# First two modulation vectors of a decoder block by quarters: sums moved from VectorE to TensorE, first norm on two engines, three projections begun quarter by quarter

## The chip, the core and the metric

One core of a Trainium2 chip runs the whole program. The metric is device time in microseconds (us) of one execution; less is better.

## The reference, cut to what matters

The program is one decoder block over 512 tokens of width 1024: adaLN modulation, two token mixers, an expert mixer and norms. The change touches only its beginning:

```python
mod = silu(c) @ w_ada + b_ada                      # c (1024), w_ada (1024, 6*1024)
shift1, scale1, gate1, shift2, scale2, gate2 = split(mod, 6)
h = rms_norm(x, norm1_w) * (1.0 + scale1) + shift1 # x (512, 1024)
proj = h @ w_in                                    # w_in (1024, 2320)
aq, ak, av, gq, gk, gv, gg, glr = split(proj)      # 512,128,128,256,256,512,512,16
log_a = log_sigmoid(glr @ gla_gate_up + gla_gate_bias) / 16
# then sliding-window attention, gated linear attention, w_out, residual,
# second norm, expert retrieval, residual, final norm
```

`h` needs all of `x` and, for each block of 128 of its 1024 columns, the same 128 columns of `scale1` and `shift1`. Everything after it is a product with `h`.

## The kernel before

All tensors have 128 partitions; a 1024-wide vector is 8 blocks (`KD`), numbered k = 0 to 7. Work is emitted in program order and a scheduler then fixes one order for each engine's queue; each queue runs strictly in that order.

The front of the program is this. SyncE (SP) issues the loads: `x` in eight pieces of 256 KB, then the columns of `w_ada` for vectors 1 (`scale1`) and 0 (`shift1`) in halves of 512 columns, 2 MB a half, and between them 1 MB groups of `w_in` (`wi3`, `wi4`, ...; group 3 is `gq`, group 4 `gk`, 0 to 2 the attention's q, k, v). The tiles of the ring `raw` (three of 1 MB) and tiles that are free so early (`qT`, `mixA`) take them.

ScalarE (ACT) squares and scales `x` (lines 233 and 237), and TensorE (PE) transposes it (`xt`, line 246; "x_transposes"). `mod_half(v, half)` makes a half of a modulation vector: VectorE (DVE) sums the 8 blocks of rows, each times `silu(c)` (`scs`), into `macc`, by one instruction of 128x512 for each block (lines 267, 269); PE then sums `macc` over the partitions by four products with a column of ones (`mt`, line 273); DVE adds the bias (`modT`, line 275) and makes `aT`, the scale of the norm (line 278).

With `aT` and `modT`, ACT turns each transposed block into `h` (line 298) and rounds it to `hTh`; DVE subtracts for the rest, `hTl` (line 302). The weights are split in the same way, `wi_0h`, `wi_1h` on ACT (line 59) and `wi_0l`, `wi_1l` on DVE (line 60), `_0` for k = 0 to 3 and `_1` for k = 4 to 7, in rings of three. A product in full precision is then three matmuls for each k (`mm3`, lines 64 to 66).

The projections are emitted in the order: the decay's gate (`decays`, accumulator `pglr`), groups 3, 4, 0, 1, 2 (`proj_T`, accumulators `pj`, two for each group: `pj30` is group 3's first). That is eleven accumulators of 8 x 3 = 24 matmuls of 512 columns, 264 in all, before the first matmul of the linear attention (`pa`, lines 474 to 493). From 340 us on, the expert mixer fills the rest of the span.

Of the kernel before, what the change touches and what calls it, by code (L numbers as in the profile page):

```python
# [17 lines left out]
P = 128  # L18
D = 1024
# [22 lines left out]
def peer_block_kernel(ctx: ExitStack, tc: tile.TileContext, a: dict, out: bass.AP):  # L42
# [9 lines left out]
    def raw(shape, name):  # L52
        return st.tile(shape, F32, tag="raw", bufs=3, name=name)
# [63 lines left out]
    def bank(name, tag="m"):  # L117
        return banks["pool"].tile([P, 512], F32, tag=tag, bufs=BUFS[tag], name=name)

    def bank2(name):  # L120
        return psf.tile([P, 2, 512], F32, tag="sc2", bufs=1, name=name)

    def pbank(name):
        return ps.tile([P, 512], F32, tag="ph", name=name)
# [104 lines left out]
    for n in range(NT):  # L229
        sq = frA.tile([P, D], F32, tag="m4", bufs=2, name=f"sqa{n}")  # L230
        ss = frA.tile([P, 2], F32, tag="ss", bufs=2, name=f"ssa{n}")
        for q in range(2):
            nc.scalar.activation(sq[:, q * 512:(q + 1) * 512], xn[n][q], AF.Square, accum_out=ss[:, q:q + 1])
        nc.vector.tensor_tensor(ss[:, 0:1], ss[:, 0:1], ss[:, 1:2], OP.add)
        r = rstd_of(frA, ss[:, 0:1], float(D), 1, f"ra{n}")
        for q in range(2):
            nc.scalar.activation(xn[n][q], xn[n][q], AF.Copy, scale=r)
    xts = []

    def x_transposes(ks):  # L240
        for k in ks:
            if k % 4 == 0:
                x_transposes.two = bank2(f"xt{k}")
            pt = x_transposes.two[:, k % 4] if k % 4 < 2 else bank(f"xt{k}", ("pt", "po")[k % 2])
            for n in range(NT):
                nc.tensor.transpose(pt[:, n * P:(n + 1) * P], xn[n][k // 4][:, k % 4 * P:(k % 4 + 1) * P], ident)
            xts.append(pt)

    x_transposes(range(4))
    hTh = frA.tile([P, KD, T], FR, name="hTh")  # L250
    hTl = frA.tile([P, KD, T], FR, name="hTl")

    mtb = bank("mt")

    def mod_half(v, half):
        acc = frA.tile([P, D], F32, tag="m4", bufs=2, name=f"macc{v}{half}")[:, :512]
        c0 = v * D + half * 512
        if v == 1:
            parts = [(raw([P, 4, 512], f"wa{half}{i}"), 4) for i in range(2)]
        else:  # L260
            parts = [(qT, 4)] + [(t.rearrange("p a b -> p (a b)")[:, None, :], 1) for t in mixA]
        k = 0
        for w, nk in parts:
            nc.sync.dma_start(w, a["w_ada"][k * P:(k + nk) * P, c0:c0 + 512].rearrange("(k p) d -> p k d", p=P))
            for i in range(nk):
                if k == 0:
                    nc.vector.tensor_scalar(acc, w[:, i, :], scs[:, 0:1], None, op0=OP.mult)
                else:
                    nc.vector.scalar_tensor_tensor(acc, w[:, i, :], scs[:, k:k + 1], acc, op0=OP.mult, op1=OP.add)
                k += 1  # L270
        pb = mtb[:, 16 * v + 4 * half:16 * v + 4 * half + 4]
        for i in range(4):
            nc.tensor.matmul(pb[:, i:i + 1], acc[:, i * P:(i + 1) * P], ones[:, 0:1], start=True, stop=True)
        cs = slice(v * 8 + 4 * half, v * 8 + 4 * half + 4)
        nc.vector.tensor_tensor(modT[:, cs], pb[:, 0:4], badaT[:, cs], OP.add)
        if v == 1:
            hs = slice(4 * half, 4 * half + 4)
            nc.vector.scalar_tensor_tensor(aT[:, 0, hs], modT[:, cs], 1.0, n1T[:, hs], op0=OP.add, op1=OP.mult)

# [6 lines left out]
    for half in range(2):  # L286
        mod_half(1, half)
        if half == 1:
            fetch(a["w_in"][4], 4, 256, "wi")
        mod_half(0, half)  # L290
        if half == 0:
            fetch(a["w_in"][3], 3, 256, "wi")
        else:
            x_transposes(range(4, KD))
        for k in range(4 * half, 4 * half + 4):
            h32 = frA.tile([P, T], F32, tag="h32", bufs=4, name=f"h32_{k}")
            if k < KD - 1:
                nc.scalar.activation(h32, xts[k], AF.Identity, bias=modT[:, k:k + 1], scale=aT[:, 0, k:k + 1])
            else:
                nc.vector.tensor_scalar(h32, xts[k], aT[:, 0, k:k + 1], modT[:, k:k + 1], op0=OP.mult, op1=OP.add)  # L300
            nc.scalar.activation(hTh[:, k, :], h32, AF.Copy)
            nc.vector.tensor_tensor(hTl[:, k, :], h32, hTh[:, k, :], OP.subtract)
    wg = frA.tile([P, KD, 16], F32, name="wg")
    nc.sync.dma_start(wg, a["w_glr"])
# [46 lines left out]
    def decays():  # L351

        pg = pbank("pglr")
        for k in range(KD):
            mm3(pg[:16, :], wgh[:, k, :], wgl[:, k, :], hTh[:, k, :], hTl[:, k, :], k == 0, k == KD - 1)
        nc.scalar.activation(glrT, pg[:16, :], AF.Copy)
        for j in range(2):
            pz = bank(f"pz{j}", ("pt", "po")[j])
# [208 lines left out]
    proj_T(4, [[t[:, :, j, :] for t in gk] for j in range(2)], bank)  # L567
# [523 lines left out]
def layouts(inp):  # L1091
# [6 lines left out]
    o["w_ada"] = c(g["w_ada"][0])  # L1098
    o["b_ada"] = c(g["b_ada"])
# [48 lines left out]
```

## Time and profile before

| what | value |
|---|---|
| median of 3 runs | 1557.18 us (1555.11 to 1562.12) |
| the profiled execution | 1555.13 us, of which its span 1553.4 us |
| TensorE busy | 1493.2 us (96%) |
| VectorE busy | 1251.8 us (81%) |
| ScalarE busy | 688.8 us (44%) |
| DMA | 409.67 MB, mean 264 GB/s |

Times inside the program are counted from the start of the span. A busy PE in these rows is not a PE at its best: matmuls overlap, so the distance between the starts of two matmuls is what one costs, and the length printed for one is longer. "idle before" stands behind a row with what ended the wait.

### The profile page before, as it was taken

The numbers are of one execution on the slowest core, as the hardware profiler recorded it, in microseconds if no ns is written. First come the engines' busy times: TensorE is split into PE (matmuls) and PEld (weight loads), VectorE is DVE, ScalarE is ACT, GpSimd is POOL, SyncE is SP. The second block draws the span as 40 slices with busy tenths as digits, with TensorE's granted clock in tenths as the row PEclk, the third lists the DMA queues.
The fourth block names the chain that finished last, engine by engine and source line by source line (L and its number), as shares of the span: only waits on it lengthen the run. The fifth ranks groups of instructions, "written<-read, shape, count | busy, mean of one in ns | idle before, by whom it ended". The sixth has DMA issues, their size and how long they took to land.

```text
span 1553.4 us, 24408 instructions
## 1 busy us (share of the span) xinstructions
PE 1493.2 (96%) x9379; PEld 1328.2 (86%) x9379; DVE 1251.8 (81%) x2476; ACT 688.8 (44%) x1078; POOL 412.9 (27%) x327
## 2 busy tenths in 40 slices
PE   4999989899999999999999999999999999999996
PEld 3787878888998999999888888888888888888885
DVE  7578668589989898995678778878888878887997
ACT  5545576433445666564333333333333333333343
POOL 1000000144500000003243334433434434434550
PEclk9999999999999999999999999999999999999998
DMA  9253444262346677679998999888998989898893
GB/s 349 89 204 131 171 142 173 108 239 92 127 155 188 198 239 235 201 239 388 380 348 317 339 348 346 322 340 333 364 330 329 338 340 354 326 340 334 292 331 129
DMA packets 154932, 409.67 MB, mean 264 GB/s; under 512 B 10288, under 2 KB 77120, under 8 KB 142400
## 3 DMA queue, kind: packets, MB, share of 16 engines
q1 hardware_dynamic: 108736, 261.30, 47.2%
q0 software_dynamic: 36864, 134.23, 23.0%
q10 hardware_dynamic: 9216, 12.59, 2.2%
q8 instruction: 73, 1.20, 0.3%
q14 instruction: 43, 0.35, 0.1%
HBM read 366.14 MB, written 41.94 MB: 263 GB/s over the span
## 4 chain that ended last, share of the span: by engine, by line
PE 63%; DVE 3%; DMA 2%; ACT 1%; issue 1%; DVEq 0%; ACTq 0%; SPq 0%
PE acc L65 11%; PE acc L64 11%; PE acc L66 11%; PE ph L66 8%; PE ph L64 8%; PE ph L65 8%; PE pg L874 4%; DMA Gd<-gs 1%; DMA gr<-Gd 1%; DVE o L867 1%; ACT gs L876 0%; DVE o L862 0%; DVE oh L819 0%; DVE oh L822 0%; DVE oh L817 0%
## 5 line engine op out<-in xcount | busy, mean ns | idle before, releaser
L887 POOL DMA_INDIRECT gu<-in_u_dram,ix_u x128 | 170.2, 1329 | 531.5 <-PE pg L874 273.5
L897 POOL DMA_INDIRECT gv<-in_vP_dram,ix_v x128 | 171.0, 1336 | 214.9 <-DVE gu L889 183.1
L902 DVE SCALAR_TENSOR_TENSOR gacc<-gv,hg,gacc 128x1024 f32<-128x1024 f32 x127 | 162.7, 1281 | 3.3 <-DMA gv<-in_vP_dram,ix_v 3.1
L889 DVE SCALAR_TENSOR_TENSOR gu<-gu,h2n 128x1024 f32<-128x1024 f32 x128 | 156.0, 1219 | 5.9 <-DMA gu<-in_u_dram,ix_u 5.9
L1028 ACT ACTIVATE Ah<-ge 128x384 fp32r<-128x384 f32 x64 | 33.6, 525 | 155.1 <-PE acc L65 155.1
L1028 ACT ACTIVATE Ah<-gel 128x384 fp32r<-128x384 f32 x64 | 33.6, 525 | 154.4 <-PE acc L65 154.4
L876 ACT ACTIVATE gs<-pg 128x512 f32<-128x512 f32 x96 | 94.3, 1108 | 9.8 <-PE pg L874 9.8
L867 DVE TENSOR_TENSOR o<-o,gp 128x1024 bf16<-128x1024 bf16 x144 | 91.0, 687 | 4.3
L874 PE MATMUL pg<-o,o 128*128 128x128 bf16 x1152 | 79.3, 223 | 5.3 <-DVE o L867 5.3
L874 PEld LDWEIGHTS <-o 128*128 128x128 bf16 x1152 | 69.7, 99 | 14.4 <-issue 8.5
L953 POOL IOTA iot<- 128x256 bf16 x1 | 1.5, 1541 | 282.8 <-DVE h2Tl L675 282.8
L1029 DVE TENSOR_TENSOR Al<-gel,Ah 128x384 fp32r<-128x384 f32 x64 | 35.6, 556 | 45.2 <-ACT Ah L1028 45.2
L699 ACT ACTIVATE ge<-ph 128x384 f32<-128x384 f32 x128 | 60.8, 475 | 23.8 <-PE ph L66 23.7
L862 DVE TENSOR_TENSOR o<-iot,t 128x2048 bf16<-128x2048 bf16 x48 | 58.5, 1218 | 4.9 <-ACT t L842 4.9
L1029 DVE TENSOR_TENSOR Al<-ge,Ah 128x384 fp32r<-128x384 f32 x64 | 35.5, 555 | 19.2 <-ACT Ah L1028 18.1
L1024 DVE TENSOR_TENSOR ge<-ge,gr 128x384 f32<-128x384 f32 x64 | 35.4, 553 | 10.9 <-ACT ge L699 10.9
L212 DVE SCALAR_TENSOR_TENSOR macc<-wa,scs,macc 128x1024 f32<-128x1024 f32 x28 | 39.0, 1392 | 4.9 <-DMA wa<-in_w_ada_dram 4.7
L1024 DVE TENSOR_TENSOR gel<-gel,gr 128x384 f32<-128x384 f32 x64 | 32.8, 553 | 0.0
L65 PE MATMUL pq<-h2Tl,wq_0h 128*128 128x512 f32 (+1 forms) x80 | 27.9, 349 | 1.2 <-DVE h2Tl L675 1.2
L64 PE MATMUL pq<-h2Th,wq_0h 128*128 128x512 f32 (+1 forms) x80 | 28.0, 352 | 1.0 <-ACT qha L751 1.0
L65 PE MATMUL pq<-h2Tl,wq_1h 128*128 128x512 f32 (+1 forms) x80 | 28.2, 353 | 0.0
L66 PE MATMUL pq<-h2Th,wq_1l 128*128 128x512 f32 (+1 forms) x80 | 28.2, 352 | 0.0
(2599 smaller groups left out, 5077.1 us busy)
## 6 DMA issues: line engine op xcount, KB each, us to landing
u<-in_uT_dram SPq DMA_DIRECT2D x64, 1024.0 KB
v<-in_vP_dram SPq DMA_DIRECT2D x64, 1024.0 KB
Gd<-gs SPq DMA_DIRECT2D x24, 1024.0 KB
gr<-Gd SPq DMA_DIRECT2D x16, 1536.0 KB
wa<-in_w_ada_dram SPq DMA_DIRECT2D x20, 1024.0 KB
gsp<-ge ACTq DMA_DIRECT2D x64, 192.0 KB
gel<-gsp SPq DMA_DIRECT2D x32, 384.0 KB
wi<-in_w_in_dram SPq DMA_DIRECT2D x9, 1024.0 KB
```

Of the source, the lines that this page charges most:

```text
L64: nc.tensor.matmul(acc, lh, rh, start=start, stop=False)
L65: nc.tensor.matmul(acc, lh, rl, start=False, stop=False)
L66: nc.tensor.matmul(acc, ll, rh, start=False, stop=stop)
L867: nc.vector.tensor_tensor(o2[:, :, m], o12[:, :, 1], gp3[:, g0:g0 + H, m, None].to_broadcast([P, H, P, 2]), OP.mult)
L874: nc.tensor.matmul(pt[:, i, :], o12[:, g, 0, :, r], o2[:, g, m, :, r], start=(m == 0), stop=(m == 2))
L876: nc.scalar.activation(gs[:, :, t0 + 4 * f:t0 + 4 * f + 4].rearrange("p b a -> p a b"), pt, AF.Copy)
L887: nc.gpsimd.indirect_dma_start(out=ur, out_offset=None, in_=a["u"], in_offset=bass.IndirectOffsetOnAxis(ap=ix_u[:, s:s + 1], axis=0))
L889: nc.vector.scalar_tensor_tensor(ur, ur, 1.0, h2n, op0=OP.mult, op1=OP.mult, accum_out=hid[:, s:s + 1])
L897: nc.gpsimd.indirect_dma_start(out=vr, out_offset=None, in_=a["vP"], in_offset=bass.IndirectOffsetOnAxis(ap=ix_v[:, s:s + 1], axis=0))
L902: nc.vector.scalar_tensor_tensor(gacc, vr, hg[:, s:s + 1], gacc, op0=OP.mult, op1=OP.add)
L1024: nc.vector.tensor_tensor(ge, ge, v_part.g[:, :, c % CG, :], OP.mult)
L1029: nc.vector.tensor_tensor(Al, gef, Ah, OP.subtract)
```

## The change

The columns of vectors 0 and 1 are laid out anew in memory, in quarters of 256 columns, so that a quarter is 1 MB with 8 KB in a row for each partition (`w_ada01`). Each vector is made by quarters (`mod_quarter`). A quarter q gives the two blocks k = 2q and 2q+1. For vector 0 and for the first quarter of vector 1, PE multiplies the raw weights with `scs`: 16 products of a 128x128 piece with one column, and DVE only adds the bias. For the other three quarters of vector 1, DVE sums as before, with 256 columns instead of 512, and PE does two products with ones. Of the first norm, DVE takes the second square and the first scaling. Transposes come by quarters in one pair of banks (`bank2`). The accumulators of the gate and of `proj_T(4)` change banks, so that the gate, `pj30`, `pj31`, `pj40` and `pj41` can all be open while the quarters arrive.

```diff
+    def mod_quarter(v, q, on_vector):
+        w = quarter.pop((v, q))
+        pb = mtb[:, 8 * v + 2 * q:8 * v + 2 * q + 2]
+        if on_vector:
+            acc = frA.tile([P, D], F32, tag="m4", bufs=2, name=f"macc{v}{q}")[:, :256]
+            nc.vector.tensor_scalar(acc, w[0], scs[:, 0:1], None, op0=OP.mult)
+            for k in range(1, KD):
+                nc.vector.scalar_tensor_tensor(acc, w[k], scs[:, k:k + 1], acc, op0=OP.mult, op1=OP.add)
+            for i in range(2):
+                nc.tensor.matmul(pb[:, i:i + 1], acc[:, i * P:(i + 1) * P], ones[:, 0:1], start=True, stop=True)
+        else:
+            for i in range(2):
+                for k in range(KD):
+                    nc.tensor.matmul(pb[:, i:i + 1], w[k][:, i * P:(i + 1) * P], scs[:, k:k + 1], start=(k == 0),
+                                     stop=(k == KD - 1))
...
+    fetch_quarter(1, 0, "A")
+    fetch_quarter(0, 0, "B")
+    fetch(a["w_in"][3], 3, 256, "wi")
+    fetch_quarter(1, 1, "C")
+    fetch_quarter(0, 1, "D")
...
+    fetch(a["w_in"][4], 4, 256, "wi")
+    fetch_quarter(1, 2, None)
...
-        for q in range(2):
-            nc.scalar.activation(sq[:, q * 512:(q + 1) * 512], xn[n][q], AF.Square, accum_out=ss[:, q:q + 1])
+        nc.scalar.activation(sq[:, 0:512], xn[n][0], AF.Square, accum_out=ss[:, 0:1])
+        nc.vector.scalar_tensor_tensor(sq[:, 512:1024], xn[n][1], 1.0, xn[n][1], op0=OP.mult, op1=OP.mult,
+                                       accum_out=ss[:, 1:2])
...
+    for q in range(4):
+        two = bank2(f"xt{q}")
+        for i in range(2):
+            k = 2 * q + i
+            for n in range(NT):
+                nc.tensor.transpose(two[:, i, n * P:(n + 1) * P], xn[n][k // 4][:, k % 4 * P:(k % 4 + 1) * P], ident)
+        mod_quarter(1, q, q > 0)
+        mod_quarter(0, q, False)
+        if q == 0:
+            fetch_quarter(0, 2, "A")
+            fetch_quarter(1, 3, "B")
+        elif q == 1:
+            fetch_quarter(0, 3, "C")
...
-    proj_T(4, [[t[:, :, j, :] for t in gk] for j in range(2)], bank)
+    proj_T(4, [[t[:, :, j, :] for t in gk] for j in range(2)], lambda name: bank(name, ("pt", "po")[int(name[-1])]))
```

What this does to the queues shows at three places. The first is PE's queue of the kernel before, where its matmuls with `h` begin. `xt6` and `xt7` are transposes of k = 6 and 7, `macc11` is the second half of vector 1; a row's numbers behind the names are those of the buffers.

```order
L246 MATMUL xt4_372<-ident_73,Eg_113 128x128 x8
L246 MATMUL xt6_381<-ident_73,Eg_113 128x128 x4
L246 MATMUL xt7_386<-ident_73,Eg_113 128x128 x4
L64 MATMUL pglr_416<-hTh_273,wgh_409 16x512
L64 MATMUL pj30_470<-hTh_273,wi3_0h_462 128x512
L65 MATMUL pglr_416<-hTl_274,wgh_409 16x512
```

All 32 transposes stand ahead of the first matmul with `h`, and of the sums over partitions (`mt`) 8 of 16 products.

The same place of PE's queue in the changed kernel, from the first matmul with `h` on; line 302 is now the transposes, line 265 the products with one column.

```order
L64 MATMUL pglr_485<-hTh_277,wgh_478 16x512
L64 MATMUL pj30_538<-hTh_277,wi3_0h_530 128x512
L64 MATMUL pj31_565<-hTh_277,wi3_0h_530 128x512
L64 MATMUL pj40_600<-hTh_277,wi4_0h_592 128x512
L64 MATMUL pj41_627<-hTh_277,wi4_0h_592 128x512
L302 MATMUL xt1_336<-ident_73,gv0_109 128x128
L302 MATMUL xt1_336<-ident_73,gv1_110 128x128
L302 MATMUL xt1_336<-ident_73,gv2_111 128x128
L302 MATMUL xt1_336<-ident_73,gv3_112 128x128
```

Behind the first five matmuls stand the eight transposes of quarter 1 and then 16 products of its vector 0; the quarters 2 and 3 follow in the same way between matmuls, so that 24 transposes and 48 products now stand behind the first matmul with `h`.

The second is one of these stretches, later in the same queue (`Eg` holds quarter 3 of vector 0).

```order
L64 MATMUL pj31_565<-hTh_277,wi3_1h_534 128x512
L65 MATMUL pj31_565<-hTl_278,wi3_1h_534 128x512
L265 MATMUL mt_276<-scs_86,Eg_113 128x1 x16
L66 MATMUL pj31_565<-hTh_277,wi3_1l_535 128x512
L64 MATMUL pj31_565<-hTh_277,wi3_1h_534 128x512
```

The 16 products stand in the middle of `pj31`, and the next matmul waits until PE has done them.

The third is DVE's queue of the changed kernel ahead of the first `h` (`macc11` and `macc12` are quarters 1 and 2 of vector 1, `wi4_0l` the lower part of `wi4`).

```order
L259 SCALAR_TENSOR_TENSOR macc11_345<-Eg_113,scs_86,macc11_345 128x256 x2
L60 TENSOR_TENSOR wi4_0l_593<-wi4_204,wi4_0h_592 128x1024
L268 TENSOR_TENSOR modT_83<-mt_276,vec_69 128x2
L257 TENSOR_SCALAR macc12_393<-wa12_206,scs_86 128x256
L314 TENSOR_SCALAR h32_1_332<-xt0_279,aT_85,modT_83 128x512
```

The bias of vector 0's first quarter (`modT`), without which there is no `h`, stands behind the split of `wi4`, and so behind that load.

On ACT, the split of `wi0` (its first half, `wi0_0h`), which needs a free place in the ring of three, now stands ahead of `h` of k = 6.

## Rows read from the trace of the kernel before

**Rows 1.** The page's busy time of PE, with its share of the span, and the clock granted to PE in 40 slices of the span.

```profile
PE 1493.2 (96%) x9379; PEld 1328.2 (86%) x9379; DVE 1251.8 (81%) x2476; ACT 688.8 (44%) x1078; POOL 412.9 (27%) x327
PEclk9999999999999999999999999999999999999998
```

**Rows 2.** Busy time by stretch: from:to and length in us, then busy us (and instructions) of PE, PEld (its weight loads), DVE, ACT, POOL, the granted clock, the DMA share and GB/s.

```profile
0.00:33.80 33.80, 11.16 (x49) 9.80 (x49) 24.83 (x80) 19.72 (x45) 4.89 (x21) 1.00 0.94 338
33.80:46.60 12.80, 10.99 (x55) 7.70 (x53) 10.02 (x18) 1.08 (x2) 0.00 (x0) 1.00 0.67 272
46.60:101.80 55.20, 55.20 (x249) 42.55 (x249) 35.34 (x55) 30.77 (x42) 0.00 (x0) 1.00 0.33 112
101.80:340.00 238.20, 225.24 (x2242) 191.82 (x2242) 171.25 (x463) 132.65 (x293) 20.30 (x10) 0.99 0.46 165
340.00:1553.40 1213.40, 1190.59 (x6791) 1076.31 (x6789) 1010.37 (x1863) 504.55 (x698) 387.70 (x297) 0.99 0.79 288
```

**Rows 3.** PE in order of time, from its first matmul with `h` to the first `pa` and one wait later: start, length, engine, line, what is written and read, count, and the idle time before it with what ended it. Between the rows at 65.27 and 70.71 lie 24 matmul starts.

```profile
33.79 0.78 PE L64 MATMUL pglr<-hTh,wgh 128*16 128x512 f32 x1
39.92 0.95 PE L273 MATMUL mt<-ones,macc 128*128 128x1 f32 x8
40.73 0.48 PE L64 MATMUL pj<-hTh,wi_0h 128*128 128x512 f32 x1
43.00 0.50 PE L66 MATMUL pj<-hTh,wi_0l 128*128 128x512 f32 x1 [1.56 <-DVE wi_0l L60]
45.40 0.95 PE L273 MATMUL mt<-ones,macc 128*128 128x1 f32 x8
46.60 0.50 PE L64 MATMUL pj<-hTh,wi_0h 128*128 128x512 f32 x1 [0.26 <-DVE modT L275]
...
60.05 1.98 PE L359 MATMUL pz<-glrT,gup 16*128 16x512 f32 x4
65.27 0.39 PE L66 MATMUL pj<-hTh,wi_1l 128*128 128x512 f32 x1
70.71 0.39 PE L66 MATMUL pj<-hTh,wi_0l 128*128 128x512 f32 x1
101.80 0.32 PE L477 MATMUL pa<-Eg 64*32 64x32 f32 x8
149.63 0.21 PE L493 MATMUL pa<-gq,gk 64*32 64x32 f32 x1 [2.11 <-issue]
```

**Rows 4.** PE in order of time: products with one column and transposes, and the row that follows where the distance is read. One product of 128x128 with one column is two records (16 products of `mt` in lines 273 are 32 records).

```profile
20.80 1.71 PE L273 MATMUL mt<-ones,macc 128*128 128x1 f32 x8
26.21 1.87 PE L273 MATMUL mt<-ones,macc 128*128 128x1 f32 x8 [3.70 <-DVE macc L269]
30.46 3.67 PE L246 MATMUL xt<-ident,Eg 128*128 128x128 f32 x16 [2.39 <-ACT h L298]
105.01 0.60 PE L575 MATMUL pv<-ident,vT 128*128 128x128 f32 x4
105.44 0.27 PE L384 MATMUL sc<-am,identb 128*128 128x256 bf16 x1
156.15 1.84 PE L224 MATMUL mt<-ones,macc 128*128 128x1 f32 x16
157.85 0.38 PE L384 MATMUL sc<-am,identb 128*128 128x512 bf16 x1
```

**Rows 5.** ACT in order of time: the split of `wi3` as it lands, and `h` and `hTh` of the first half.

```profile
25.20 1.06 ACT L59 ACTIVATE wi_0h<-wi 128x1024 fp32r<-128x1024 f32 x1 [5.38 <-DMA wi<-in_w_in_dram]
28.96 2.79 ACT L298 ACTIVATE h<-xt,modT,aT 128x512 f32<-128x512 f32 x4 [1.56 <-DVE modT L275]
31.63 2.19 ACT L301 ACTIVATE hTh<-h 128x512 fp32r<-128x512 f32 x4
```

**Rows 6.** DVE in order of time: three blocks of a half's sum, the lower part of `wi3`, and a bias.

```profile
17.92 2.33 DVE L269 SCALAR_TENSOR_TENSOR macc<-wa,scs,macc 128x512 f32<-128x512 f32 x3
26.29 1.23 DVE L60 TENSOR_TENSOR wi_0l<-wi,wi_0h 128x1024 fp32r<-128x1024 f32 x1
28.77 0.15 DVE L275 TENSOR_TENSOR modT<-mt,vec 128x4 f32<-128x4 f32 x1
```

**Rows 7.** Busy time by stretch, columns as in rows 2, while the first loads run.

```profile
10.00:20.00 10.00, 3.45 (x13) 2.25 (x14) 6.82 (x25) 7.34 (x19) 0.00 (x0) 1.00 1.05 392
20.00:30.00 10.00, 4.38 (x21) 4.20 (x19) 9.65 (x17) 3.24 (x5) 0.00 (x0) 1.00 1.05 389
30.00:40.00 10.00, 9.54 (x42) 7.19 (x42) 9.79 (x16) 4.88 (x8) 0.00 (x0) 1.00 1.04 408
```

**Rows 8.** Busy time by stretch, columns as in rows 2, behind the wait of 2.11 us in rows 3.

```profile
150.00:151.00 1.00, 1.00 (x9) 0.97 (x9) 1.00 (x2) 0.26 (x1) 0.00 (x0) 0.94 0.82 315
151.00:152.00 1.00, 1.00 (x7) 1.00 (x6) 1.00 (x2) 0.34 (x1) 0.00 (x0) 0.50 0.04 12
153.00:154.00 1.00, 1.00 (x6) 1.00 (x6) 1.00 (x4) 0.97 (x5) 0.00 (x0) 0.50 0.65 147
154.00:155.00 1.00, 1.00 (x11) 0.87 (x12) 1.00 (x2) 1.00 (x6) 0.00 (x0) 0.85 1.06 438
```

**Rows 9.** What PE waited for from 101.8 to 340 us, the longest: us in total, times, longest.

```profile
PE pa L493 <- issue: 2.8, 2, 2.1
PE pn L64 <- ACT Eg L348: 1.6, 1, 1.6
```

## What I expected, before the changed kernel was run

> **What bounds the kernel now.** I read the page first: TensorE (PE) is busy 96% of the span [rows 1], so what counts is where PE stands still, or does work that it need not do. The table of stretches says where [rows 2]: PE is busy 11.2 of the first 33.8 us, 11.0 of the next 12.8, all of the 55.2 us from 46.6 to 101.8, 225 of 238 us to 340, and 1191 of 1213 us after that. So PE waits for the rest of the machine only until 46.6 us; from there the front of the program is a PE queue. Anything that puts more work into that queue, or takes some out, moves the end by as much, unless one of the few later waits takes it up.
>
> The timeline of PE over this stretch [rows 3] gives the yardstick. PE starts with `h` at 33.79 and reaches `pa` at 101.80, 68.0 us later. The 264 matmuls of 512 columns in between cost 5.44 us / 24 = 0.2267 us each, 59.85 us together. All else in these 68.0 us is 8.15 us: the two groups of `mt` and their surroundings, the wait of 1.56 for `wi_0l`, the two `pz` (1.98), a slow first microsecond. The old way thus wastes little once it has begun: what there was to win is the 33.8 us before, and some 4 us of waits and sums behind them.
>
> **When PE starts in the changed kernel.** The loads bind until then: 389 to 408 GB/s in every stretch of ten us [rows 7]. Before, `wi3` is the seventh megabyte in line (2 of `x`, 4 of `w_ada`, itself), and ACT starts on it as it lands, at 25.20 [rows 5]. In the new order the seventh megabyte is quarter 1 of vector 0, and `wi4` follows with the small `wg` ahead of it: 1.11 MB more, 2.8 us at 390 GB/s, so 28.0; I take 27.6, since half of the new pieces lie 8 KB in a row and the rate was 408 where more such groups ran. Then come in line, by the queues shown with the change: ACT's split of `wi4` (1.06 long, about 1.0 until the next) [rows 5], DVE's lower part (1.23, about 1.1), the bias (0.15) [rows 6], `h` (2.79/4 = 0.70) and `hTh` (2.19/4 = 0.55) [rows 5], and some 0.3 for four hand-overs. Together 3.8: PE begins with `h` at 31.4, 2.4 us earlier than before. DVE's and ACT's work is hidden behind the loads otherwise: the four squares and scalings that DVE takes over lie before 20 us, and the sums of vector 0 that it loses (two halves of 8 instructions, 0.75 to 0.78 each [rows 6], some 12 us) did not sit ahead of PE after 46.6. Of the waits only 1.56 + 0.26 [rows 3] go with them.
>
> **What PE's queue then holds.** The same 264 matmuls, 59.85. Of the transposes, 24 instead of none. They cost 0.11 each where PE runs at its upper clock ((105.44 - 105.01)/4) and 0.23 where it doesn't (3.67/16) [rows 4]; at the upper level 2.6 us. Then 48 products with one column (three quarters of vector 0, 16 each). The trace has such products: `mt` at 156.15, 8 products in 16 records, is followed 1.70 us later, so 0.2125 each; earlier, at 20.80 and 26.21, 4 took 1.71 and 1.87, so 0.45 [rows 4]. At the upper level the 48 are 10.2 us. Two sums with ones, two products each: 0.85. The two `pz`: 1.9. One new wait: ACT's split of `wi0` needs a place in the ring that PE frees only in the middle of quarter 3, and `h` of k = 6 stands behind it on ACT; by my count PE comes to that `h` some 1.0 us before it is there (0 to 2). Sum beside the 264: 16.55 against 8.15, so 8.4 us more, less the 2.4 of the earlier start: **6.0 us later at `pa`**, with PE at its upper clock throughout. I checked the other side of each step on the way: quarter 3 of vector 1 is the last load; 5.4 MB behind `wi4` at 400 GB/s it lands near 41, and its `h` is wanted by PE some 20 us later (31.4 and the two thirds of 27.2 + 16.6 that stand ahead of it), so no load is late for PE any more. That is the point of the change, and it is paid with PE time.
>
> **The clock.** [...] The granted column reads 1.00 before 34 us, but the transposes at 30.46 and the products at 20.80 cost twice what the same forms cost at 105 and 156 [rows 4], so this is the lower level. Later the column shows one fall: after a standstill of 2.11 us [rows 3] it reads 0.50 at 151 to 154 and is back in the slice after [rows 8]: some 3.4 us at half pace, 1.7 us lost. In the changed kernel PE does only products and eight transposes, with gaps between loads, until 31.4, so I expect it to start low: five matmuls at 0.43 and eight transposes at 0.23 instead of 0.2267 and 0.11 are 2.0 us more. Whether a stretch of 16 products keeps PE up, no row shows: the longest in the trace is the 1.70 us at 156, with no fall. Bounds for each of the three stretches: nothing, or 16 x (0.45 - 0.2125) = 3.8 in it and 1.7 behind it. That gives 0 to 2.0 + 3 x 5.5 = 18.5 us in all. I take 5.0: the slow start, and one stretch of the three, for a stretch of 3.4 us with hardly a column streaming is nearer to the standstill than to the matmuls around it, yet lies between full work.
>
> **Sum.** 6.0 + 5.0 = 11.0 us later at `pa`. From 101.8 to 340 us PE stands 13 us, and nearly all of these waits are for results that PE's own queue feeds (the longest that are not are 1.6 us for ACT and the 2.8 of "issue" [rows 9]); I let none of it absorb the delay, 4 at most. The profiled execution of 1555.13 (span 1553.4) becomes 1566.1; it lies 2 below the median 1557.18, which becomes **1568**. This measurement can tell about 0.5%, 7.8 us, from no change.
>
> **Rivals.**
> A, the forecast: PE's queue grows, 1562 to 1575, **0.5**.
>
> B, the clock falls in every stretch. Then up to 6.0 + 18.5 = 24.5 us, 1575 to 1582. For it: the fall after 2.11 us of standstill [rows 8]. Against it: no fall after 1.70 us of products. **0.15**. [...]
>
> C, no change: the delay is taken up after `pa`. DVE has 12 us less to do early, the scheduler's order between 100 and 230 us differs in many places, and waits there could shrink. At +4 or less the result is 1555 to 1562, **0.2**. Against it: nothing before 340 us but PE is near its limit (DVE 171 of 238 us, ACT 133 [rows 2]).
>
> D, faster: the products cost PE nothing, because their weight loads slip behind the 512-column matmuls around them (PEld is busy only 42.6 of 55.2 us there [rows 2]). The sum beside the 264 falls to some 3.8 with transposes free too: 31.4 + 63.6 = 95.0, 6.8 us earlier than before, 1550; with waits after `pa` shrinking too, 1544. It decides at the price of a product: below 4.2/48 = 0.088 us the change wins, above it loses. The row says 0.2125, inside dense work [rows 4]. [...] **0.15**, which also holds what I don't see in the new order.
>
> **Numbers.** 1568 is A. A's own range is 1562 to 1575; the range 1553 to 1580 takes in C, most of B and the upper half of A's absorption, and leaves out D and the ends. Faster by over 0.5% (below 1549): part of D, 0.12. Slower by over 0.5% (above 1565): B and most of A, 0.6. Within 0.5%: 0.28.
>
> **What would show it.** In the profile after: PE's first matmul with `h` between 30 and 33; the three groups of 32 records of one-column products at 3.4 us each or up to 7; hardly any wait of PE from there to `pa`; `pa` at 107 to 115. `pa` before 101.8 refutes the sum. With `pa` at 108 or later and an end that is not later, C holds. I am wrong if the products are cheaper than 0.1 us, if PE starts with `h` before 28, or if PE waits for loads in the middle.

## The result, and the profile after

The changed kernel takes 1576.49 us (median of 5 runs, 1575.72 to 1576.91) against 1557.18 before: ratio 1.0119, 95% interval 1.0103 to 1.0135, so slower by 19.3 us. The profiled execution took 1576.91, its span is 1575.1; before it was 1553.4, so the two traces differ by 21.7. Of e6, one of the kernels further down, two executions took 3810 and 8377 us; they are left out of its median and ratio.

The page of after, PE's busy time and granted clock, answers to [rows 1]: PE is busy 27 us more, a point more of a longer span, and the clock's second slice is now an 8.

```profile
PE 1520.2 (97%) x9519; PEld 1353.0 (86%) x9519; DVE 1250.2 (79%) x2489; ACT 678.9 (43%) x1060; POOL 408.3 (26%) x327
PEclk9899999999999999999999999999999999999999
```

The stretches of after, columns as in [rows 2], cut at PE's first matmul with `h`, at the first `pa` (right behind the last `pj`), and at the first `ph`. That is an early matmul of the expert mixer: its work on PE begins with `pq`, some 24 us ahead of `ph`, and so well before the 340 us named at the head of this document. Under them the last two stretches of before, cut at the same places (the first of its stretches, 33.79 to 101.80, can be read from [rows 3]).

```profile
31.67:117.09 85.42, 85.42 (x397) 68.50 (x397) 44.86 (x84) 33.74 (x45) 0.00 (x0) 0.92 0.31 113
117.09:317.70 200.61, 185.89 (x1998) 154.26 (x1998) 139.49 (x310) 112.00 (x266) 1.87 (x2) 0.97 0.43 149
317.70:1575.10 1257.40, 1231.74 (x7052) 1114.02 (x7050) 1045.10 (x2019) 520.12 (x722) 401.80 (x304) 0.99 0.79 286
```

```profile
101.80:295.90 194.10, 181.14 (x1983) 151.69 (x1983) 136.60 (x307) 116.65 (x269) 1.87 (x2) 0.98 0.43 152
295.90:1553.40 1257.50, 1234.69 (x7052) 1116.44 (x7050) 1045.01 (x2019) 520.55 (x722) 406.13 (x304) 0.99 0.79 286
```

So there are two losses and no third. In the **front**, PE starts 2.1 us earlier, needs 85.4 instead of 68.0 us for the eleven accumulators, and is done 15.3 later. In the **middle**, up to the first `ph`, another 6.5 are lost (200.6 against 194.1), 1.8 of them with PE standing (14.72 against 12.96) and 4.8 with PE busy longer over nearly the same matmuls (1998 and 1983 records). Behind `ph` nothing moves (1257.4 and 1257.5).

PE of after in order of time, answering to [rows 3]: the products of the first quarter of vector 0, ahead of `h`; the start; the three stretches of products with the row that follows each; and the first `pa` behind the last `pj`. The last row is DVE's: the bias of that first quarter.

```profile
22.96 6.98 PE L265 MATMUL mt<-scs,mixA 128*128 128x1 f32 x32 [0.73 <-DVE modT L268]
...
31.67 0.61 PE L64 MATMUL pglr<-hTh,wgh 128*16 128x512 f32 x1 [0.46 <-ACT hTh L317]
32.07 1.91 PE L64 MATMUL pj<-hTh,wi_0h 128*128 128x512 f32 x4
33.78 1.91 PE L302 MATMUL xt<-ident,gv 128*128 128x128 f32 x8
35.48 1.39 PE L265 MATMUL mt<-scs,wakl 128*128 128x1 f32 x8
...
39.41 0.39 PE L65 MATMUL pglr<-hTl,wgh 128*16 128x512 f32 x1
...
50.00 3.65 PE L265 MATMUL mt<-scs,qT 128*128 128x1 f32 x32
53.51 0.77 PE L66 MATMUL pj<-hTh,wi_0l 128*128 128x512 f32 x1
...
64.27 4.23 PE L265 MATMUL mt<-scs,Eg 128*128 128x1 f32 x32
68.36 0.77 PE L66 MATMUL pj<-hTh,wi_1l 128*128 128x512 f32 x1
...
117.09 0.45 PE L489 MATMUL pa<-Eg 64*64 64x64 f32 x8
...
29.98 0.16 DVE L268 TENSOR_TENSOR modT<-mt,vec 128x2 f32<-128x2 f32 x1 [0.42 <-PE mt L265]
```

The three stretches take 3.93, 3.51 and 4.09 us, 11.53 together. Around the first and the third, by stretch, columns as in [rows 2]; PE is busy all the time.

```profile
38.00:39.00 1.00, 1.00 (x11) 1.00 (x11) 0.00 (x0) 0.00 (x0) 0.00 (x0) 1.00 1.09 414
40.00:43.00 3.00, 3.00 (x9) 1.95 (x8) 2.35 (x6) 1.89 (x3) 0.00 (x0) 0.50 0.36 147
43.00:44.00 1.00, 1.00 (x6) 0.82 (x5) 0.96 (x3) 0.00 (x0) 0.00 (x0) 0.89 0.00 0
66.00:67.00 1.00, 1.00 (x11) 1.00 (x11) 0.00 (x0) 0.00 (x0) 0.00 (x0) 1.00 0.00 0
70.00:73.00 3.00, 3.00 (x8) 2.32 (x8) 1.64 (x3) 0.80 (x2) 0.00 (x0) 0.50 0.00 0
74.00:75.00 1.00, 1.00 (x6) 0.73 (x5) 0.66 (x1) 0.00 (x0) 0.00 (x0) 1.00 0.00 0
```

The granted clock (the last column but two) reads 1.00 within the products and drops to 0.50 around their end: the matmuls of 512 columns behind them then stand 0.43 apart instead of 0.2267, and pay for it. [Rows 8] showed such a fall behind a standstill of 2.11 us; here there is no standstill at all. The front adds up: 59.85 for the 264 matmuls, 11.53 for the products, 3.32 for 24 transposes (1.70 + 0.79 + 0.83), 0.72 for two sums, 2.10 for two `pz`, 0.98 for the first five matmuls (2.11 us, 0.42 apart instead of 0.2267); that is 78.50 of 85.42. The remaining 6.9 are the falls; the clock column gives the same, (1 - 0.92) x 85.42 = 6.8. (It reads 1.00 in the slow start, so it holds the falls alone.)

In the middle, the longest wait of after is new: `gb`, the sum of the third modulation vector, waits 4.3 us for ACT's copy `gv` ([rows 9] have none such). PE, then ACT in order of time, then two stretches.

```profile
150.82 2.08 PE L219 MATMUL gb<-macc,ones 128*128 128x512 f32 x2 [4.27 <-ACT gv L362]
...
146.90 3.60 ACT L461 ACTIVATE Eg<-Eg 128x4096 f32<-128x4096 f32 x1
150.41 0.36 ACT L362 ACTIVATE gv<-pn 128x256 f32<-128x256 f32 x1
...
148.00:149.00 1.00, 0.00 (x0) 0.00 (x0) 1.00 (x3) 1.00 (x1) 0.00 (x0) 1.00 0.00 0
150.00:155.00 5.00, 4.18 (x13) 3.15 (x14) 4.51 (x15) 0.77 (x2) 0.00 (x0) 0.50 0.52 192
```

`gb` needs a bank of the ring of two in which `pn` is summed, and the copy that frees it stands behind an exponential of 3.60 us in ACT's queue. Behind the wait the clock is down again (0.50 from 150 to 155).

### The profile page after: what moved, and what is told of

Read it like the earlier page. It is cut to its first block, busy times and chain, and to the rows that moved or that the text cites. A ratio compares the mean times of both kernels' runs of the same rounds, so it can differ in the third digit from the quotient of the medians.

```text
span 1575.1 us, 24684 instructions
## 1 busy us (share of the span) xinstructions
PE 1520.2 (97%) x9519; PEld 1353.0 (86%) x9519; DVE 1250.2 (79%) x2489; ACT 678.9 (43%) x1060; POOL 408.3 (26%) x327
## 4 chain that ended last, share of the span: by engine, by line
PE 62%; DVE 3%; DMA 2%; ACT 1%; issue 1%; DVEq 0%; SPq 0%; ACTq 0%
PE acc L65 11%; PE acc L64 11%; PE acc L66 11%; PE ph L66 8%; PE ph L64 8%; PE ph L65 8%; PE pg L889 4%; DMA Gd<-gs 1%; DMA v<-in_vP_dram 1%; DVE o L882 1%; ACT gs L891 0%; DVE oh L834 0%; DVE o L877 0%; DVE oh L832 0%; DMA u<-in_uT_dram 0%
```

## The experiments

Twelve kernels, each timed beside the kernel before on its own chip. Theory 1 of those that cure the front (e1, e2, e5): one-column products cost their own time, and a stretch of them makes the clock fall behind it. The other theories, and the rivals, are named in each expectation. "Front" is from PE's first matmul with `h` to the first `pa`, "middle" from there to the first `ph`; idle is PE's in the middle, clock the granted clock there. All of these are read from one traced execution of each kernel, while the median is over all its executions; the traced one lies between 5.7 us below its median (e2) and 5.6 above (e11).

| kernel | first `h` | front | middle | idle | clock | first `ph` | median | ratio to before (95%) |
|---|---|---|---|---|---|---|---|---|
| before | 33.79 | 68.0 | 194.1 | 13.0 | 0.98 | 295.9 | 1557.2 | |
| after | 31.67 | 85.4 | 200.6 | 14.7 | 0.97 | 317.7 | 1576.5 | 1.0119 (1.0103 to 1.0135) |
| e1, sums by DVE | 31.88 | 70.6 | 203.2 | 14.0 | 0.93 | 305.7 | 1565.0 | 1.0036 (1.0019 to 1.0052) |
| e2, rows | 31.33 | 81.8 | 191.9 | 12.2 | 1.00 | 305.0 | 1567.4 | 1.0059 (1.0041 to 1.0076) |
| e3, before + norm | 33.52 | 67.8 | 196.2 | 13.4 | 0.97 | 297.5 | 1557.4 | 0.9998 (0.9984 to 1.0012) |
| e4, `gb` own bank | 31.39 | 87.6 | 196.0 | 12.6 | 0.98 | 315.0 | 1575.8 | 1.0107 (1.0085 to 1.0129) |
| e5, interleaved | 31.17 | 77.8 | 202.2 | 15.7 | 0.96 | 311.2 | 1576.6 | 1.0118 (1.0101 to 1.0135) |
| e6, e5 + first rows | 26.60 | 78.7 | 203.1 | 15.4 | 0.94 | 308.4 | 1567.2 | 1.0076 (1.0048 to 1.0103) |
| e7, e1 + first rows | 28.24 | 82.1 | 203.2 | 18.4 | 0.96 | 313.5 | 1572.5 | 1.0087 (1.0068 to 1.0105) |
| e8, e7 + `gb` | 28.84 | 80.9 | 208.3 | 19.7 | 0.93 | 318.0 | 1577.6 | 1.0117 (1.0098 to 1.0137) |
| e9, all rows | 27.09 | 84.2 | 210.0 | 16.5 | 0.93 | 321.2 | 1579.0 | 1.0146 (1.0124 to 1.0168) |
| e10, e5 + `gb` | 31.24 | 79.0 | 201.6 | 15.6 | 0.96 | 311.8 | 1573.3 | 1.0102 (1.0086 to 1.0119) |
| e11, e1 + `gb` | 31.69 | 70.8 | 213.8 | 17.6 | 0.89 | 316.2 | 1572.3 | 1.0090 (1.0074 to 1.0107) |
| e12, before + `gb` | 33.89 | 67.6 | 205.6 | 16.7 | 0.94 | 307.1 | 1566.0 | 1.0054 (1.0038 to 1.0070) |

### The products taken off TensorE

```diff
-        mod_quarter(0, q, False)
+        mod_quarter(0, q, q > 0)
```

> The changed kernel, but the quarters 1 to 3 of vector 0 are summed by VectorE, like those of vector 1; TensorE does two products with ones for each. Theory 1 (the three stretches of 16 one-column products cost their own time and make the clock fall behind each): the stretches of 3.93, 3.65 and 4.23 us and the falls behind them (about 6.6 us together) go, three pairs of products come (about 1.2), so the first `pa` moves from 117.1 to about 100 and the time from 1576.5 to 1559 or 1560. Theory 2 (the clock falls for another reason, the low start or the transposes): only the stretches' own time goes, `pa` near 106.5, falls still there, about 1566. Rival 3 (VectorE becomes late with 24 more sums of about 0.4 us between 25 and 65 us): TensorE waits for `modT` or `hTl` in that stretch, `pa` at 103 to 110, 1562 to 1570.

PE of this kernel, its start, the end of the front, and two places in the middle, with a stretch of the clock.

```profile
31.88 0.61 PE L64 MATMUL pglr<-hTh,wgh 128*16 128x512 f32 x1 [0.46 <-ACT hTh L317]
102.16 0.39 PE L66 MATMUL pj<-hTh,wi_1l 128*128 128x512 f32 x1
112.30 0.48 PE L508 MATMUL pa<-gq,gk 64*32 64x32 f32 x27 [4.01 <-issue]
159.36 3.57 PE L224 MATMUL mt<-ones,macc 128*128 128x1 f32 x16
...
158.00:168.00 10.00, 10.00 (x69) 7.62 (x67) 8.75 (x14) 1.54 (x3) 0.00 (x0) 0.50 1.00 340
```

Two sums with ones and no product stand in the way, and the front shrinks by 14.8 us; `pa` comes at 102.5, between theory 1 (100) and its rival (106.5), since PE now waits 1.7 for `hTh` within the front (rival 3, but small). Theory 1 holds for the front. The middle lost 2.6 us again, with a standstill of 4.01 us and 20 us at a granted clock of 0.50 (158 to 178). The end of the traced execution is 15.3 earlier all the same, as the stretch behind `ph` came out 3.3 shorter; the median gained only 11.5, and where the other runs lost the rest was not traced. And even without one product in PE's way the front is 2.6 longer than in the kernel before, by the 24 transposes, the slow start (five matmuls in 2.11 us) and the wait for `hTh`; that is more than the 1.9 us that PE starts earlier, so `pa` still comes 0.7 later than before.

### The same sums with columns that stream

```diff
+        elif v == 0 and q > 0:
+            rw = mtb[0:1, 16:272]
+            for k in range(KD):
+                nc.tensor.matmul(rw, scs[:, k:k + 1], w[k], start=(k == 0), stop=(k == KD - 1))
+            row = frA.tile([1, 256], F32, tag="row", bufs=2, name=f"row{q}")
+            nc.vector.tensor_copy(row, rw)
+            for i in range(2):
+                nc.tensor.matmul(pb[:, i:i + 1], row[0:1, i * P:(i + 1) * P], ones[0:1, 0:1], start=True, stop=True)
```

> The changed kernel, but for the quarters 1 to 3 of vector 0 the product is turned round: 8 products with `scs` as the weights and 256 columns streaming, into one row, which VectorE copies out and two tiny products turn into columns. Same data, about the same own time (a product of 256 columns in full precision about 0.45 us at the upper clock, half the 128x512 one of `gb`, so 3.6 us a stretch). Theory 1 (a stretch in which hardly a column streams is what lets the clock fall): no fall behind the stretches, `pa` at about 110.5 instead of 117.1, about 1570. Theory 2 (the falls come from something else): falls as before, `pa` near 117, 1575 to 1577.

One stretch of row products, the end of the front, and the clock over front and middle.

```profile
47.98 3.62 PE L265 MATMUL mt<-qT,scs 128*1 128x256 f32 x16
112.81 0.39 PE L66 MATMUL pj<-hTh,wi_1l 128*128 128x512 f32 x1
...
31.33:113.00 81.67, 80.86 (x360) 57.48 (x360) 45.76 (x87) 33.52 (x45) 0.00 (x0) 1.00 0.32 119
113.00:305.00 192.00, 179.85 (x2000) 149.72 (x1999) 139.70 (x310) 115.40 (x269) 1.87 (x2) 1.00 0.45 156
```

The stretch costs what it did (3.62 against 3.51), and no fall follows any of the three (the clock reads 1.00): the form decides, theory 1 holds. `pa` is 4.0 earlier (113.13), not the 6.6 expected (110.5); 0.8 went into two waits (PE busy 80.86 of 81.67), about 1.6 into the three pairs of tiny products (the matmul behind the first pair starts 0.53 later). The median fell by more than the front, 9.1 us, since the middle of this order of work is the shortest of all.

### The norm alone

```diff
-            nc.scalar.activation(xn[n][q], xn[n][q], AF.Copy, scale=r)
+        nc.vector.tensor_scalar(xn[n][0], xn[n][0], r, None, op0=OP.mult)
+        nc.scalar.activation(xn[n][1], xn[n][1], AF.Copy, scale=r)
```

(the second square moves in the same way.)

> The kernel before with the split of the first norm over two engines alone. My account (TensorE's start hangs on the loads and the sums, not on the norm): first matmul with `h` at 33.8 within 0.4, time 1557 within 2. Rival (the norm's share of the front is what the change gains or loses): start 1 us or more earlier or later, and the time with it.

PE starts at 33.52, and the time is 1557.4, as I held: the norm's split is worth nothing here that can be measured.

### The wait of `gb`

```diff
-                pb = pbank(f"gb{v}{q}")
+                gb2 = bank2(f"gb{v}") if q == 0 else gb2
+                pb = gb2[:, q]
```

> The changed kernel, but the two sums of the third vector over the partitions (`gb`) go to a pair of banks that is free by then instead of the ring of two that the `pn` accumulators use. Theory 1 (part of the loss behind `pa` is the wait of 4.3 us of `gb` for ScalarE's `gv`, with the clock fall behind it that costs another 2.8): both go, 4 to 6 us earlier from 160 us on, 1571 to 1573. Rival (the next `pn` needs the same place in the ring, so the wait only moves by a microsecond): 1575 to 1577.

In the trace the wait and its fall are gone (clock 1.00 from 140 to 180) and the middle is 4.6 us shorter, as theory 1 said. The median is not (1575.8, the rival's range): in the profiled execution the front was 2.2 longer (its first product stretch took 6.68 us instead of 3.93, with a clock column of 1.00 from 30 to 50) and the part behind `ph` 2.8. This one trace does not settle which of these the other runs had.

### The products between matmuls

```diff
+    after = lambda b, a: tc.add_manual_dep(b.ins, a.ins.name, mybir.DependencyInfo(
+        mybir.DependencyClass.NoSync, mybir.DependencyReason.DATA), reason="interleave")
+    for q in range(1, 4):
+        xs = [x for i, x in enumerate(byk[q - 1]) if q > 1 or i % 6][:16]
+        for j, x in enumerate(xs):
+            after(x, prods[0, q][j])
+            if j:
+                after(prods[0, q][j], xs[j - 1])
```

(`byk` holds the matmuls of the open accumulators by quarter, `prods` the products.)

> The changed kernel with the same 48 products of the quarters 1 to 3 of vector 0, but no longer in three stretches of 16: issue-order edges put one product between two of the first 16 or so matmuls of 512 columns of the quarter before. Nothing else is changed. Theory 1 (the clock falls behind a stretch in which hardly a column streams, and the price of 0.2125 stands): no fall, last `pj` at 116.8 - 6.6 = about 110, time about 1569. Rival D of the prediction in its second chance (weight loads of single products slip behind the matmul ahead of them): besides, a product costs less than 0.1, so 48 x 0.11 or more go too: last `pj` near 104.5, 1562 to 1564. Rival 3 (one-column products let the clock fall wherever they stand, or TensorE pays for each change between forms): last `pj` at 116 or later, 1575 or more.

Five rows in the middle of the first stretch, the end of the front, and the front as one stretch.

```profile
34.86 0.40 PE L65 MATMUL pglr<-hTl,wgh 128*16 128x512 f32 x1
35.10 0.28 PE L266 MATMUL mt<-scs,wakl 128*128 128x1 f32 x2
35.23 0.39 PE L66 MATMUL pglr<-hTh,wgl 128*16 128x512 f32 x1
...
37.15 0.47 PE L66 MATMUL pj<-hTh,wi_0l 128*128 128x512 f32 x1
37.60 0.48 PE L64 MATMUL pj<-hTh,wi_0h 128*128 128x512 f32 x1
...
108.65 0.39 PE L66 MATMUL pj<-hTh,wi_1l 128*128 128x512 f32 x1
...
31.17:108.97 77.80, 77.74 (x397) 63.00 (x397) 44.40 (x84) 33.42 (x45) 0.00 (x0) 1.00 0.34 127
```

The same 397 records as after, 7.6 us less, clock 1.00: the falls are gone, and with them a little more than the 6.9 us that the sum above puts down to them. A pair of matmul and product takes 0.37 beside `pglr` and 0.45 beside `pj`, so 0.14 and 0.23 for the product. Beside `pj` that is the price that the prediction had, beside `pglr` a third less; both lie above the 0.1 that rival D needed, so D is refuted. But the end again did not follow: the median is 1576.6. The profiled run was the shortest (1572.0), with a new wait of 4.7 us of `pt` for ACT in the middle and a clock of 0.96 there.

### An earlier start

```diff
+        elif q == 0:
+            rw = mtb[0:1, 16 + 240 * v:272 + 240 * v]
```

(then as in the kernel with rows; the rest is the interleaved kernel.)

> As the interleaved kernel, and the two first quarters (q = 0 of vectors 1 and 0), which TensorE makes ahead of its first matmul with `h`, are turned round too: 8 products of 256 streaming columns each, a copy of the row by VectorE, two tiny products. Theory 1 (the slow start of about 2 us comes from one-column products ahead of it, which leave the clock at its lower level): 16 products of 0.22 to 0.43 each no longer keep it down; the first matmuls with `h` run at 0.227 apart, last `pj` 1.5 to 2 us earlier than in the interleaved kernel. Rival (the low start comes from the gaps while the loads run): matmuls of 512 columns still 0.43 apart until about 35 us, and the start itself about 0.5 to 1 later for the copy and the tiny products; last `pj` equal or up to 1 later.

The sum ahead of the first `h`, that matmul, and the clock behind it.

```profile
19.97 3.61 PE L265 MATMUL mt<-mixA,scs 128*1 128x256 f32 x16 [0.25 <-DVE modT L277]
26.60 0.61 PE L64 MATMUL pglr<-hTh,wgh 128*16 128x512 f32 x1 [1.91 <-ACT hTh L326]
27.00:30.00 3.00, 3.00 (x15) 2.69 (x13) 3.00 (x5) 1.32 (x2) 0.00 (x0) 0.54 0.98 384
```

Neither theory had it right. The row form takes 3.61 us where the products had taken 6.98, so PE starts 4.6 us earlier; but it then stands 1.91 us, and the granted clock behind that is 0.54. The last `pj` comes 3.7 earlier (104.97), by the start alone. Here the slow start stands behind a standstill, with no more than two tiny products (0.60 us) ahead of it; whether standstills or one-column products make the start of the other kernels slow stays open.

### Both cures, the same with `gb`, and rows everywhere

These three put the edits above together: rows for the first quarters with the sums of the others by DVE (below), that with `gb` in its own banks, and rows for every quarter that PE sums (`elif True` in place of the condition, and the call as in the changed kernel).

```diff
+        elif q == 0:
+            rw = mtb[0:1, 16 + 240 * v:272 + 240 * v]
...
-        mod_quarter(0, q, False)
+        mod_quarter(0, q, q > 0)
```

> The changed kernel with both cures of its front: the two first quarters as 8 products of 256 streaming columns (as in the interleaved kernel with rows, which began with `h` at 26.6 instead of 31.2), and the quarters 1 to 3 of vector 0 summed by VectorE (no products in the way of the matmuls). Theory 1 (the front is a TensorE queue, and what is in it decides): start near 26.6, last `pj` near 97 to 99 (102.16 where VectorE summed and the start was 31.88, less 5.3, less what VectorE comes late with); if the stretch behind it takes 192 to 203 us, as in the kernels so far, 1547 to 1560, so as fast as the kernel before or faster. Rival (VectorE with 48 sums is late for every quarter after so early a start): waits of TensorE for `hTh` of 2 us a quarter, last `pj` at 102 or later, 1560 to 1566.

> The same with the sums of the third vector in a pair of banks of their own. Theory (the wait of `gb` for ScalarE's `gv` and the clock fall behind it cost 3 to 5 us behind `pa` in this order of work too): 3 to 5 faster than the kernel with the two cures alone, if that one shows the wait. Rival (other waits and falls take its place behind `pa`, as in the first run of this edit, where the trace gained 4.6 us up to the first `ph` and the median nothing): equal within 2.

> The changed kernel with all five quarters that TensorE sums as products of 256 streaming columns, three of them in the way of its matmuls. Theory 1 (the products' own time stays, the clock does not fall): start near 26.6, last `pj` at 112.81 - 4.7 = about 108, 1560 to 1566. If instead the stretch behind `pa` decides (it took 192.2 us in the profile of the kernel with rows, where no fall was seen, and 200 to 203 in the others), it shows here again whether that was the form of the products or chance: 192 to 195 for the form, 200 or more for chance.

My expectation for the first failed by 11 us at the last `pj` (109.97 against 97 to 99). Two of PE's starts on a new quarter in e7, and the clock behind the second.

```profile
40.77 0.40 PE L64 MATMUL pglr<-hTh,wgh 128*16 128x512 f32 x1 [1.79 <-ACT hTh L325]
53.48 0.61 PE L64 MATMUL pglr<-hTh,wgh 128*16 128x512 f32 x1 [2.80 <-ACT hTh L325]
54.00:58.00 4.00, 4.00 (x15) 3.03 (x14) 4.00 (x10) 0.63 (x1) 0.00 (x0) 0.50 0.01 4
```

Started at 28, PE outruns DVE's sums: it stands 7.6 us in the front, 6.3 of them in three waits for `hTh`; behind the one of 1.79 the clock stays at 1.00, behind those of 2.80 and 1.72 it falls (0.50 at 54 to 58, 0.57 over 66 to 70). The rival had the mechanism, but not the time (1572.5 against its 1560 to 1566). The edit of `gb`, worth 4.6 us in the middle of after, made the middle 5.1 longer here, and e8 is 5 slower than e7, which neither of its theories had. And rows everywhere show that the 191.9 of the first kernel with rows was not the form's doing: 210.0 now. Its last `pj` came at 110.92 instead of about 108, its time is 13 above the range expected, and it is the slowest of all.

### The two single cures together, and a control

All three have the edit of `gb` shown above, in the interleaved kernel, in the one with sums by DVE, and in the kernel before.

> The interleaved kernel with the sums of the third vector in a pair of banks of their own: both single cures (8.1 us earlier at the last `pj`, 4.6 us less from there to the first `ph`) in one kernel. Each left the median where it was (1576.6 and 1575.8 against 1576.5). Theory 1 (the two add up, and what the medians hid were other waits and clock falls behind `pa` that come with each order of work): last `pj` at 108 to 109, first `ph` at 303 to 306, 1563 to 1567. Rival (the kernel behind `pa` takes up what comes early: a standstill and a fall in the place of each that is taken away): first `ph` at 310 or later, 1572 to 1577.

> The kernel with the quarters of vector 0 summed by VectorE, with the third vector's sums in their own banks. Its last `pj` stood at 102.16, its first `ph` at 305.7, 203.5 later. Theory 1 (what it lost behind `pa` was chance of order): a number between 192 and 203 for that stretch, most of all near 198, and 1555 to 1562. Rival (it gets worse, as in the kernel with early rows, where the same edit made the stretch 5 longer): 1565 to 1570.

> A control: the kernel before with the same small edit behind `pa` and nothing else. Its first product with `h` and its last `pj` cannot move by more than 0.5. What the stretch from there to the first `ph` does (194.4 before) shows how much an order of work alone moves the time where nothing is added and nothing taken away. Theory 1 (the scheduler's order there is worth several us either way, by its standstills and the clock falls behind them): 190 to 200 and a time of 1553 to 1563. Rival (the order behind `pa` is robust in the kernel before, and only the later, denser front of the changed one upsets it): within 1 of 194.4, within 2 of 1557.

The first gave 1573.3: the rival's outcome. In the second the middle grew by 10.5 between the two traces, and the median is 1572.3, beyond both theories; by the medians it is 7 or 8 us slower than e1, half of what the traces say. The third is the one that explains, though it too went beyond its theory 1 (200 and 1563): the kernel before, with the two sums moved to another bank. Start, end of its front, the place where the middle goes wrong, and the clock behind it.

```profile
33.89 0.47 PE L64 MATMUL pglr<-hTh,wgh 128*16 128x512 f32 x1
101.17 0.39 PE L66 MATMUL pj<-hTh,wi_1l 128*128 128x512 f32 x1
155.73 0.79 PE L64 MATMUL pn<-wi_0h,hTh 128*128 128x256 f32 x2 [4.34 <-ACT wi_0h L59]
...
156.00:166.00 10.00, 10.00 (x42) 7.60 (x42) 9.64 (x15) 2.81 (x7) 0.00 (x0) 0.50 0.88 304
```

The front is that of before within 0.4 us, and the kernel is slower by 8 or 9 us (ratio 1.0054, interval 1.0038 to 1.0070). Nothing was added; the scheduler's order in the middle came out differently, PE stands 4.34 us for a split that waits for its load, and the granted clock stays at 0.50 for some 20 us. Over all fourteen kernels the middle holds nearly the same matmuls (1983 to 2000 records) and takes 191.9 to 213.8 us. Length less idle less (1 - clock) x length is 173 to 180 in each of them, and lowest where the middle is longest (e11): standstills and the clock make up the spread, though this simple sum charges the low clock with some us too many. In this kernel, then, the order behind the front can cost about half of what the change cost.

## Why the prediction was right in its direction and where it was off

**The start.** 31.4 forecast, 31.67 measured, but not quite by the steps named. ACT began to split `wi4` as it landed, at 27.25 (27.6 forecast), and DVE was done with its part at 29.56; the bias that `h` waits for came 0.42 later, released by PE's products for it. These took 6.98 us, 0.44 each, and stand nowhere in the sum. In e6, where they take 3.61 and DVE makes the bias ahead of that split, PE starts at 26.60: so this load bound the start only by the order of DVE's queue, and the good number is in part luck. **No load late for PE** held: PE is busy 85.42 of 85.42 us.

**The queue.** 16.55 us beside the 264 matmuls were forecast, 17.67 measured: products 11.53 (10.2), transposes 3.32 (2.6), sums 0.72 (0.85), `pz` 2.10 (1.9), the wait for ACT's ring 0 (1.0). Products and transposes are over by the slow ones: the first eight transposes took 1.70 us against 0.79 and 0.83, the first and third stretch 3.93 and 4.09 against 3.51. The price of 0.2125 for a product was right: 3.51/16 = 0.219 in the second stretch, the fastest of the three. PEld is busy all of the two slices inside a stretch (1.00 of 1.00 us at 38 and at 66), against 0.73 among dense matmuls at 74; that these products are weight loads and little else is argued from this, not shown.

**The clock: the term that was mis-sized.** I took 5.0, the slow start and one fall in three. All three stretches were followed by a fall: 6.9 us behind them, 0.98 in the first five matmuls, and some 1.8 in the excess of transposes and products, 9.7 in all. The step that failed is the choice of one stretch in three, between two far ends: three fell, at 1.7, 1.7 and 3.4 us by the clock column. The only row near, 1.70 us of products with no fall [rows 4], did not speak for stretches of 3.5 us. Rival B had the mechanism; its upper bound was too high for this execution, because inside a stretch a product cost 0.219 to 0.256, not 0.45, and the fall came behind it. (In the trace of e4 the first stretch did take 6.68 us, 0.42 each.) The same form as in [rows 4], 8 products in 16 records, ran at 159.36 in e1 and took 3.57 us, at a clock already down (0.50). The fall behind the wait of 4.27 us of `gb` came behind a standstill, like that in [rows 8]; the falls of the front came with no gap at all (PE busy 85.42 of 85.42 us). The trace of after shows no low clock in the slow start: the column reads 1.00 there, and that it is low is read from the price alone (0.42 a matmul); behind the standstills ahead of the starts of e6 and e7 the column does show it (0.54 at 27 to 30, 0.50 at 30 to 32).

**Nothing absorbed: only half the question.** I let the middle absorb nothing, "4 at most", and gave it no way to add. It added 6.5. I had seen that the order differs there in many places, and made of it only rival C, a gain. The control shows that it can be a loss of 11 us there (205.6 against 194.1) for no work at all. In after itself, 4.6 of the 6.5 went with the wait of `gb` (e4). Of the 21.7 us between the traces, 15.3 are the front's (11.0 forecast) and 6.5 the middle's (none forecast).

**The end.** The sum said 11 and the medians say 19.3. The result lies in the range and in the direction that I gave most weight, by the price of B and a loss behind `pa` that B did not hold; A's own range, 1562 to 1575, missed it by 1.5. The forecast of 1568 was 8.5 too low, by two errors of the same sign (in the traces 4.3 in the front and 6.5 in the middle); that the whole range held is owed to its width. `pa` at 117.09 lies outside the 107 to 115 that I named as its test. C and D are refuted, D by the price of products between matmuls (0.14 to 0.23 against the 0.088 at which it would have begun to win).

**What stays open.** Two cures were shown in the front (falls removed, 7.6 us; products removed, 14.8), and each end gained less than its front: 0 and 11.5 in the medians. The rows of e2 went the other way, 3.6 in the front and 9.1 in the median. That e5's middle lost time by order is read from its one trace; why its other runs were up to 5 us longer than that one was not traced. No version here beats the kernel before.

## What to carry to other kernels

When work is moved onto an engine that is the queue from some point on, price it on that queue; before, these sums were made by an engine with time to spare while the loads ran (DVE was busy 24.8 of the first 33.8 us [rows 2]). Where one-column products must stand among dense matmuls, try them one by one between the matmuls, or turned so that columns stream: here a turned stretch cost about the same (3.62 against 3.51 us), and in neither form did the clock fall behind it (1.00 over the fronts of e2 and e5). And before a gain of half a per cent is credited to an edit, make a control that only disturbs the scheduler's order: here it was worth 8 or 9 us.

## What was not expected of the hardware

The granted clock stayed at 0.50 for 20 us with PE busy throughout (e1, 158 to 178; e12, 156 to 176), while in the front of after, in dense matmuls of 512 columns, it came back after 3.4 us in the first two falls and after 6.8 in the third, by the clock column; both long cases hold 8 one-column products and many short matmuls, and what decides was not isolated.

PE's longest waits without a releaser ("issue") in the middle stand in or behind the bursts of some 150 small `pa` matmuls. Those of 3.3 us and more (in e1, e7, e8, e9 and e11) all stand where the loads fill the DMA engines (share 0.91 to 1.03); where these idle, none read here is above 1.2. First e7, then after, each with the stretch that shows the DMA share (the last but one column).

```profile
120.19 0.25 PE L516 MATMUL pa<-gq,gk 64*32 64x32 f32 x3 [3.87 <-issue]
118.00:120.00 2.00, 0.00 (x0) 0.00 (x0) 0.50 (x1) 1.06 (x1) 0.00 (x0) 1.00 1.03 377
...
140.29 0.21 PE L505 MATMUL pa<-Eg 64*32 64x16 f32 x3 [0.27 <-issue]
140.00:141.00 1.00, 0.73 (x42) 0.72 (x41) 0.69 (x2) 0.90 (x2) 0.00 (x0) 1.00 0.00 0
```

The DMA table shows one packet (0.02 MB) of a queue that it calls "instruction" beside the burst in both. That the instructions themselves come late through full queues is argued from this, not shown.
